# HGRN2 score levels: the two finest ones written after the value projection, apart from the others, with the transposes between them and one shared buffer

## The chip, the cores and the metric

The kernel runs on one core of a Trainium2 chip. A core has a matrix engine (TensorE; PE for its matmuls, PEld for the loads of the stationary operand), a vector engine (VectorE; DVE), a scalar engine (ScalarE; ACT), GpSimd (POOL) and SyncE (SP), which only starts transfers. The metric is the device time of one execution in microseconds (us), lower is better; the kernel before is given by the median of three runs.

## What is computed

One layer of a decoder trunk for 1024 prompt tokens and 64 sample tokens (8 sequences of 8), so 1088 columns in all. Four token mixers share one input projection, and an MLP follows. The change touches one of the four, HGRN2, a gated linear recurrence with four heads of 128 x 128 state. From the reference, cut:

```python
def step(s, inp):
    qi, ki, fi, vi = inp
    b = jnp.cumsum(fi, axis=2)
    o_inter = jnp.einsum("bhtd,bhdv->bhtv", qi * jnp.exp(b), s)
    diff = b[:, :, :, None, :] - b[:, :, None, :, :]
    decay = jnp.exp(jnp.where(causal, diff, -jnp.inf))
    scores = jnp.sum(qi[:, :, :, None, :] * ki[:, :, None, :, :] * decay, axis=-1)
    o = o_inter + jnp.einsum("bhts,bhsv->bhtv", scores, vi)
    b_last = b[:, :, -1:, :]
    s_new = jnp.exp(b_last[:, :, 0, :])[..., None] * s + \
        jnp.einsum("bhsd,bhsv->bhdv", ki * jnp.exp(b_last - b), vi)
    return s_new, o
```

The decay depends on the channel, so the scores of a chunk are not one product of two matrices.

## The kernel before

**Stages.** Tokens lie along the free axis, channels on the 128 partitions. A first stage norms and modulates the input into `Hh` and `Hl`, the high and low parts of a two-part split. The mixer stage follows, up to about 1475 us of the trace, then the branch products, the output product and the MLP. Each projection (`gemm`, L174) is 8 k-blocks x 3 column chunks x 3 products (high-high, low-high, high-low), 72 matmuls of some 363 columns, all recorded on the helper line L107 with the tiles `pg<-Hh,whi` and so on. Its weights come in two halves, each loaded by SP into `wst`, copied by ACT into `whi` and subtracted by DVE into `wlo`.

**Order.** The mixer stage has four rounds, `ROUNDS` (L1087): a string of letters, each of which runs one step of a generator. `r` is a step of RWKV-7, `h` of HGRN2, `c` and `l` of the two convolution branches, `g` a gate projection as filling work, `a` a piece of the conditioning. A round ends in `...h...g h h` (in the last one with the letters a little moved), so each head of HGRN2 has four steps: the q projection; the f projection and all levels of scores; the V projection; the output-gate projection and the rest. What is written is not the final order: at compile time a scheduler puts the instructions of each engine in order, by the place in the program as priority (weights and evacuations of projections have a higher one), whatever is ready by its own model of times first. On the chip each engine then takes its list strictly in that order.

**`hg_block` (L755), one call for each head.** After the projections, `b` (tile `hlf`) is the running sum of the log decay by chunks of 128 tokens (scan, L774). The 128 x 128 scores of a chunk are built by levels. For the level `hs` the chunk falls into groups of `2*hs` tokens, and a tile `X` holds, in the lower half of each group, `exp(b_ref - b) * k`, in the upper half `exp(b - b_ref) * q`, with `b_ref` the value at the group's middle: two DVE subtracts (L809, L810), one ACT exp (L811), two DVE products (L812, L813). A product of the two halves then gives the scores across the middle. Levels 64 and 32 go to the PSUM tiles `l64` and `l32` and by ACT into `P` (tile `hP`). Levels 16, 8, 4, 2 and the two base cases (tokens with themselves and with their neighbour) go through `small_level` (L784): 64 or 68 matmuls of 32 columns each into a PSUM tile `lv`, and one or two predicated copies of DVE (L791, L794) into `acc` (tile `hacc`). When all levels are in, POOL copies the diagonal blocks of `acc` into `P` and `Ps` (L834, L836).

After the next two projections the rest follows: `eb = exp(b)`, `q *= eb` (L847), the decayed keys `kd` (L848 to L854), then a loop over `c0` = 0, 4, 8 (L859) that transposes `V` and `kd` by TensorE into the PSUM tile `htr` (L867, L868), copies them by ACT to `VT`, multiplies `VT` with `P` into `po` and with itself into the state sums `hs`, and carries the state `hS` through four chunks by DVE.

**Buffers.** `flat(name, slot)` (L117) gives one of 13 buffers of 128 x 1120 floats; two tiles with one slot share it, and the later waits until all readers of the earlier are done. The slots of `X` are 3, 12, 7, 3, 12, 7 for the levels 64 to 2. `VT` has 7, 3, 7 for `c0` = 0, 4, 8; the output `hy` has 12. PSUM tiles of `pmt` (`lv`, `l64`, `l32`, `htr`, `hs`) share three banks.

Of the kernel before, what the change touches and what calls it, by code (L numbers as in the profile page):

```python
# [14 lines left out]
OP = mybir.AluOpType  # L15
# [6 lines left out]
NT = T + NS * TS  # L22
# [68 lines left out]
class Net:  # L91
# [70 lines left out]

    def products(self, ps, n0, n, W, X, k0, kt, nk=4):

        hi, lo = W
        xh, xl = X
        for k in range(k0, k0 + nk):
# [5 lines left out]

    def gemm(self, ap, kt, X, evac, chunks=CHUNKS):  # L174
        pss = [None] * len(chunks)
        for k0 in range(0, kt, 4):
            W = self.weights(ap[:, k0:k0 + 4, :])
            for i, (n0, n) in enumerate(chunks):
                if k0 == 0:
                    pss[i] = self.pgt("pg")  # L180
                self.products(pss[i], n0, n, W, X, k0, kt)
                if k0 + 4 == kt:
                    with self.tc.high_priority(offset=PRIO):
                        evac(pss[i], n0, n)

    def gemm_quarters(self, parts, X, evac, groups):


        pss = [None] * len(groups)
        xh, xl = X  # L190
        for j, (ap, ks) in enumerate(parts):
# [563 lines left out]
    def hg_block(self, h):  # L755
        nc = self.nc
        lb, om = self.hlb[:, 8 + h:9 + h], self.hlb[:, 12 + h:13 + h]
        q, f, k = (self.flat(n, i) for n, i in (("hq", 4), ("hf", 1), ("hk", 2)))
# [18 lines left out]
        acc = self.hp.tile([128, 9, 32], F32, name="hacc")  # L777
        P_t = self.flat("hP", 10)
        P = P_t[:, 0:T].rearrange("p (c t) -> p c t", t=128)
        Ps = P_t[0:64, T:NT]  # L780
# [18 lines left out]
        nc.gpsimd.tensor_copy(x1[:, ev], k[:, ev])  # L799
        self.tt(x1[:, od], q[:, od], f[:, od], OP.mult)  # L800
        small_level(4, x1, x1, True)
        for hs in (64, 32, 16, 8, 4, 2):
            N = NT if hs <= 4 else T
            v = lambda a: a[:, :N].rearrange("p (g t) -> p g t", t=2 * hs)
            ng = N // (2 * hs)
            X = self.flat("X", {64: 3, 32: 12, 16: 7, 8: 3, 4: 12, 2: 7}[hs])
            lo, hi = slice(0, hs), slice(hs, 2 * hs)
            ref = v(b)[:, :, hs - 1:hs].to_broadcast([128, ng, hs])
            self.tt(v(X)[:, :, lo], ref, v(b)[:, :, lo], OP.subtract)  # L809
            self.tt(v(X)[:, :, hi], v(b)[:, :, hi], ref, OP.subtract)  # L810
            self.act(X[:, :N], X[:, :N], AF.Exp)  # L811
            self.tt(v(X)[:, :, lo], v(X)[:, :, lo], v(k)[:, :, lo], OP.mult)  # L812
            self.tt(v(X)[:, :, hi], v(X)[:, :, hi], v(q)[:, :, hi], OP.mult)  # L813
            if hs == 64:
                ps = self.pmt("l64")
                for c in range(8):
                    o = c * 128
                    self.mm(ps[0:64, c * 64:c * 64 + 64], X[:, o:o + 64], X[:, o + 64:o + 128])
                self.act(P[0:64, :, 64:128], c3(ps[0:64, :]))
            elif hs == 32:  # L820
                ps = self.pmt("l32")
                for c in range(8):
                    for g in range(2):
                        o = c * 128 + 64 * g
                        self.mm(ps[64 * g:64 * g + 64, c * 32:c * 32 + 32], X[:, o:o + 64], X[:, o + 32:o + 64])
                for g in range(2):
                    R = slice(64 * g, 64 * g + 32)
                    self.act(P[R, :, 64 * g + 32:64 * g + 64], ps[R, :256].rearrange("p (c t) -> p c t", t=32))
            else:
                small_level(HLV.index(hs), X, X, hs <= 4)  # L830

        for g in range(4):
            R = slice(32 * g, 32 * g + 32)
            nc.gpsimd.tensor_copy(P[R, :, R], acc[R, 0:8, :])  # L834
            if g < 2:
                nc.gpsimd.tensor_copy(Ps[R, R], acc[R, 8, :])  # L836

        yield
        V = self.flat("hV", 6)
        self.proj(8 + h, lambda ps, n0, n: self.act(V[:, n0:n0 + n], ps[:, :n]))  # L840
# [3 lines left out]

        eb = self.flat("eb", 1)
        self.act(eb[:, :NT], b[:, :NT], AF.Exp)
        self.tt(q[:, :NT], q[:, :NT], eb[:, :NT], OP.mult)  # L847
        kd = self.flat("kd", 9)  # L848
        for sl, L in ((slice(0, 1024), 128), (slice(1024, NT), 8)):
            v = lambda a: a[:, sl].rearrange("p (c t) -> p c t", t=L)  # L850
# [3 lines left out]
        self.tt(kd[:, :NT], kd[:, :NT], k[:, :NT], OP.mult)  # L854

        ident = self.c("ident")
        y = self.flat("hy", 12)
        S = None
        for c0 in (0, 4, 8):  # L859
            w = 4 if c0 < 8 else 1  # L860
            VT = self.flat("VT", (7, 3, 7)[c0 // 4])[:, :1024].rearrange("p (c a t) -> p c a t", a=2, t=128)
            for c in range(c0, c0 + w, 2):
                ps = self.pmt("htr")
                if c < 8:
                    for cc in range(2):
                        o = (c + cc) * 128
                        nc.tensor.transpose(ps[:, cc * 256:cc * 256 + 128], V[:, o:o + 128], ident)  # L867
                        nc.tensor.transpose(ps[:, cc * 256 + 128:cc * 256 + 256], kd[:, o:o + 128], ident)  # L868
                    self.act(VT[:, c - c0:c - c0 + 2].rearrange("p c a t -> p (c a t)"), ps)
                else:  # L870
                    nc.tensor.transpose(ps[0:64, 0:128], V[:, 1024:NT], ident)
                    nc.tensor.transpose(ps[0:64, 128:256], kd[:, 1024:NT], ident)
                    self.act(VT[0:64, 0].rearrange("p a t -> p (a t)"), ps[0:64, :256])
            po = self.py.tile([128, 512], F32, name="po", tag="py")
            if c0 < 8:
                for c in range(c0, c0 + 4):
# [4 lines left out]
            if c0 < 8:  # L881
# [3 lines left out]
                for c in range(c0, c0 + 4):  # L885
# [8 lines left out]
                    S = Sn  # L894
# [657 lines left out]
```

## Time and profile before

| what | us |
| --- | --- |
| median of 3 runs | 2525.07 |
| the three runs | 2525.07, 2526.18, 2517.87 |
| the profiled execution | 2528.64 |
| its span, first to last instruction | 2526.9 |

The page of the profile gives the busy time of each engine over the span, the span in 40 slices, the transfers by queue, the chain of work that ended last, and the costliest groups of instructions. Other views answer questions on the same trace: waits of an engine by what ended them, instructions in order of time (neighbours of one kind merged into one row, with the idle time before it in brackets and what ended that), and the busy time of the engines in chosen stretches with the TensorE clock that was granted there (1.00 is full speed). "issue" as the end of a wait means that the engine waited for nothing that the profile shows. A matmul's end is modelled and matmuls overlap, so the pace of TensorE is read from the distance of their starts.

The four calls of `hg_block` have their levels at about 383 to 410, 719 to 750, 1060 to 1090 and 1406 to 1438 us of the span. They are called rounds 0 to 3 below.

### The profile page before, as it was taken

Reading aid. Unit: us, or ns where it says so; the run is one execution under the profiler, and the core shown is the slowest. Engines: PE = TensorE matmul, PEld = TensorE weight load, DVE = VectorE, ACT = ScalarE, POOL = GpSimd, SP = SyncE. Lnnn points to the kernel's source line nnn. Section 1 sums busy time; section 2 is a strip of 40 time slices with the busy share of each in tenths; the row PEclk is TensorE's granted clock in tenths of the full one; section 3 lists DMA queues with packets and bytes.
Section 4 is the critical chain, followed back from the end, with each engine's and each line's share of the span. In section 5 each row is a group of like instructions: output and inputs, shape, how many; then the busy total and the mean of one; then the engine's idle time right before and its main releaser. Section 6 shows DMA issues by size and latency. Waiting matters only on the chain.

```text
span 2526.9 us, 46611 instructions
## 1 busy us (share of the span) xinstructions
PE 2430.2 (96%) x19086; PEld 2255.0 (89%) x19086; DVE 1381.1 (55%) x2536; ACT 1037.1 (41%) x1855; POOL 330.2 (13%) x503
## 2 busy tenths in 40 slices
PE   6999999999999999999999999998899999999996
PEld 2897899898888988989888899998899999999996
DVE  6664626637365555457553667668755552422247
ACT  4512434323454235442244653346666665111115
POOL 3101210103100021101012000000222221000003
PEclk9999999999999999999999999999999999999998
DMA  6323132223221232112313455533565557434144
GB/s 242 120 85 91 56 104 68 70 74 98 92 68 63 81 97 97 68 62 80 98 60 105 163 186 169 194 114 104 157 157 157 157 153 257 137 139 184 61 158 132
DMA packets 185111, 300.46 MB, mean 119 GB/s; under 512 B 57385, under 2 KB 97273, under 8 KB 184897
## 3 DMA queue, kind: packets, MB, share of 16 engines
q1 hardware_dynamic: 134480, 217.79, 27.1%
q0 software_dynamic: 47104, 74.44, 9.7%
q10 hardware_dynamic: 3312, 5.25, 0.6%
q8 instruction: 150, 2.46, 0.4%
q14 instruction: 65, 0.52, 0.1%
HBM read 211.29 MB, written 81.66 MB: 116 GB/s over the span
## 4 chain that ended last, share of the span: by engine, by line
PE 79%; DVE 9%; DMA 6%; issue 3%; ACT 3%; SPq 0%; DVEq 0%; ACTq 0%; POOL 0%; POOLq 0%
PE pg L107 52%; PE pa L107 6%; PE pe L107 4%; PE sm L107 2%; PE pc L107 2%; PE pb L107 2%; PE ada L107 2%; PE pu L107 2%; DMA zx<-At 1%; DVE X L101 1%; DVE wlo L101 1%; PE G L107 1%; DMA adaw<-ada 1%; PE pyr L107 1%; PE po L107 1%
## 5 line engine op out<-in xcount | busy, mean ns | idle before, releaser
L107 PE MATMUL pg<-Hh,whi 128*128 128x362 f32 (+1 forms) x1872 | 631.5, 338 | 3.4 <-ACT Hh L98 3.1
L107 PE MATMUL pg<-Hh,wlo 128*128 128x362 f32 (+1 forms) x1872 | 632.6, 338 | 0.0
L107 PE MATMUL pg<-Hl,whi 128*128 128x362 f32 (+1 forms) x1872 | 625.2, 336 | 0.7 <-DVE Hl L104 0.6
L98 ACT ACTIVATE whi<-wst 128x512 fp32r<-128x512 f32 (+1 forms) x404 | 249.9, 620 | 617.0 <-PE pg L107 542.1
L101 DVE TENSOR_TENSOR wlo<-wst,whi 128x512 fp32r<-128x512 f32 (+1 forms) x404 | 280.3, 695 | 379.6 <-ACT whi L98 378.8
L107 PEld LDWEIGHTS pg<-Hh,whi 128*128 128x128 f32 x1872 | 357.4, 191 | 18.9 <-ACT Hh L98 5.9
L107 PEld LDWEIGHTS pg<-Hh,wlo 128*128 128x128 f32 x1872 | 357.8, 191 | 11.9 <-issue 4.2
L107 PEld LDWEIGHTS pg<-Hl,whi 128*128 128x128 f32 x1872 | 356.8, 191 | 10.1 <-issue 2.5
L107 PE MATMUL pg<-ah,whi 128*128 128x272 f32 x960 | 275.3, 289 | 4.3 <-ACT whi L98 4.3
L107 PE MATMUL pg<-ah,wlo 128*128 128x272 f32 x960 | 276.4, 290 | 0.6 <-DVE wlo L101 0.6
L107 PE MATMUL pg<-al,whi 128*128 128x272 f32 x960 | 273.0, 289 | 0.0
L107 PEld LDWEIGHTS pg<-ah,whi 128*128 128x128 f32 x960 | 180.9, 189 | 5.1 <-ACT whi L98 4.9
L107 PEld LDWEIGHTS pg<-ah,wlo 128*128 128x128 f32 x960 | 181.1, 189 | 1.6 <-DVE wlo L101 1.4
L107 PEld LDWEIGHTS pg<-al,whi 128*128 128x128 f32 x960 | 179.4, 189 | 0.0
L104 DVE SCALAR_TENSOR_TENSOR cacc<-u,pv,cacc 128x1024 f32<-128x1024 f32 x120 | 153.7, 1280 | 2.0
L104 DVE SCALAR_TENSOR_TENSOR R<-pg,mod,R 128x544 f32<-128x544 f32 (+2 forms) x120 | 65.7, 569 | 133.8 <-PE pg L107 133.8
L107 PE MATMUL pg<-yh,whi 128*128 128x362 f32 (+1 forms) x384 | 128.7, 335 | 0.9 <-DVE gt L101 0.9
L107 PE MATMUL pg<-yh,wlo 128*128 128x362 f32 (+1 forms) x384 | 127.5, 332 | 0.0
L107 PE MATMUL pg<-yl,whi 128*128 128x362 f32 (+1 forms) x384 | 127.1, 331 | 0.0
L1177 POOL DMA_DIRECT2D g<-gst x96 | 53.3, 555 | 399.0 <-ACT gst L98 383.5
L98 ACT ACTIVATE gst<-pg 128x362 f32<-128x362 f32 (+1 forms) x96 | 45.3, 472 | 134.8 <-PE pg L107 122.5
L689 POOL TENSOR_SCALAR sp<-St,dec 128x64 f32<-128x64 f32 x60 | 56.1, 935 | 231.0 <-DVE St L104 209.1
(446 smaller groups left out, 4819.3 us busy)
## 6 DMA issues: line engine op xcount, KB each, us to landing
wst<-w SPq DMA_DIRECT2D x136, 256.0 KB, 3.2
wst<-w_in SPq DMA_DIRECT2D x92, 256.0 KB, 2.8
gt<-g SPq DMA_DIRECT2D x32, 544.0 KB, 3.7
wst<-w_gate SPq DMA_DIRECT2D x64, 256.0 KB, 2.9
adaw<-ada SPq DMA_DIRECT2D x32, 512.0 KB, 5.3
ah<-ah POOLq DMA_DIRECT2D x60, 272.0 KB, 2.7
al<-al POOLq DMA_DIRECT2D x60, 272.0 KB, 4.3
ah<-ah SPq DMA_DIRECT2D x30, 544.0 KB, 10.0
```

The costliest lines, as they stand in the source:

```text
L98: return self.nc.scalar.activation(out, in_, func, bias=bias, scale=scale)
L101: return self.nc.vector.tensor_tensor(out, a, b, op=op)
L104: return self.nc.vector.scalar_tensor_tensor(out, a, s, b, op0=op0, op1=op1)
L107: return self.nc.tensor.matmul(out, lhsT, rhs, start=start, stop=stop, skip_group_check=True)
L689: nc.gpsimd.tensor_scalar(sp, St, dec[:, c:c + 1], None, op0=OP.mult)
L1177: nc.gpsimd.dma_start(d[:, n0:n0 + n], t[:, :n])
```

## The change

The body of the loop over levels becomes a function `level(hs)`, and the transposes a function `transposes(c0)`. Levels 64, 32, 16 and 8 stay where they were. Levels 4 and 2 are written after the output-gate projection and the decayed keys: transposes of chunks 0 to 3, level 4, transposes of chunks 4 to 7, level 2, and only then POOL's copies into `P` and `Ps` and the product `q *= eb`. The `X` of level 2 has slot 12 now, that of level 4, and no longer slot 7. The loop over `c0` takes the two `VT` that are already there and transposes only the sample tokens itself. The instructions are the same in kind and number, and so are all sizes.

```diff
-        for hs in (64, 32, 16, 8, 4, 2):
+        def level(hs):
             N = NT if hs <= 4 else T
...
-            X = self.flat("X", {64: 3, 32: 12, 16: 7, 8: 3, 4: 12, 2: 7}[hs])
+            X = self.flat("X", {64: 3, 32: 12, 16: 7, 8: 3, 4: 12, 2: 12}[hs])
...
-        for g in range(4):
-            R = slice(32 * g, 32 * g + 32)
-            nc.gpsimd.tensor_copy(P[R, :, R], acc[R, 0:8, :])
-            if g < 2:
-                nc.gpsimd.tensor_copy(Ps[R, R], acc[R, 8, :])
-
+        for hs in (64, 32, 16, 8):
+            level(hs)
         yield
...
         self.act(eb[:, :NT], b[:, :NT], AF.Exp)
-        self.tt(q[:, :NT], q[:, :NT], eb[:, :NT], OP.mult)
         kd = self.flat("kd", 9)
...
-        y = self.flat("hy", 12)
-        S = None
-        for c0 in (0, 4, 8):
+        def transposes(c0):
             w = 4 if c0 < 8 else 1
             VT = self.flat("VT", (7, 3, 7)[c0 // 4])[:, :1024].rearrange("p (c a t) -> p c a t", a=2, t=128)
             for c in range(c0, c0 + w, 2):
...
+            return VT
+
+        VTs = []
+        for c0, hs in ((0, 4), (4, 2)):
+            VTs.append(transposes(c0))
+            level(hs)
+        for g in range(4):
+            R = slice(32 * g, 32 * g + 32)
+            nc.gpsimd.tensor_copy(P[R, :, R], acc[R, 0:8, :])
+            if g < 2:
+                nc.gpsimd.tensor_copy(Ps[R, R], acc[R, 8, :])
+
+        self.tt(q[:, :NT], q[:, :NT], eb[:, :NT], OP.mult)
+        y = self.flat("hy", 12)
+        S = None
+        for c0 in (0, 4, 8):
+            VT = VTs[c0 // 4] if c0 < 8 else transposes(c0)
```

## The prediction

> **What bounds the kernel now.** I read the page first, then what TensorE waits for, then its instructions in time around the levels, and last the granted clock there.
>
> ```profile
> span 2526.9 us, 46611 instructions
> PE 2430.2 (96%) x19086; PEld 2255.0 (89%) x19086; DVE 1381.1 (55%) x2536; ACT 1037.1 (41%) x1855; POOL 330.2 (13%) x503
> q8 instruction: 150, 2.46, 0.4%
> ```
>
> TensorE is busy for 96% of the span, so the change can only pay by idle or slow time of TensorE; work of DVE, ACT and POOL counts where TensorE waits for it. The third row is wanted below: 150 transfers of instructions, 2.46 MB, so 16.4 KB each. TensorE has 2 x 19086 instructions, and 38172 / 150 = 254: this queue brings TensorE's code in blocks of about 256 instructions.
>
> The waits of TensorE, by line and by what ended them:
>
> ```profile
> PE lv L107 <- issue: 9.2, 5, 3.0
> ...
> PE lv L107 <- DVE X L101: 1.9, 3, 0.8
> ```
>
> So the small-level matmuls `lv` stand idle 9.2 us in five pieces without waiting for any engine, and only 1.9 us for DVE. In order of time the five are these (start, duration, count, and in brackets the idle time before):
>
> ```profile
> 405.52 1.64 PE L107 MATMUL lv<-X 128*32 128x32 f32 x140
> 407.68 0.73 PE L107 MATMUL lv<-X 128*32 128x32 f32 x60 [0.53 <-issue]
> ...
> 720.70 0.77 PE L107 MATMUL lv<-x 128*32 128x32 f32 x67 [0.21 <-DVE x L101]
> 722.45 0.19 PE L107 MATMUL lv<-x 128*32 128x32 f32 x1 [0.98 <-issue]
> ...
> 742.28 1.73 PE L107 MATMUL lv<-X 128*32 128x32 f32 x167
> 747.02 0.66 PE L107 MATMUL lv<-X 128*32 128x32 f32 x33 [3.02 <-issue]
> ...
> 1082.82 2.10 PE L107 MATMUL lv<-X 128*32 128x32 f32 x194
> 1087.33 0.33 PE L107 MATMUL lv<-X 128*32 128x32 f32 x6 [2.41 <-issue]
> ...
> 1430.06 1.40 PE L107 MATMUL lv<-X 128*32 128x32 f32 x132
> 1433.08 0.75 PE L107 MATMUL lv<-X 128*32 128x32 f32 x64 [0.43 <-DVE X L101]
> 1436.15 0.32 PE L107 MATMUL lv<-X 128*32 128x32 f32 x4 [2.32 <-issue]
> ```
>
> Four of the five lie in the run of levels 8, 4 and 2: 64 + 68 + 68 = 200 matmuls, 400 instructions with their loads, at about 12 ns a matmul (167 in 1.73 us is 10). Each time the stall comes at another place of the run, after 140, 167, 194 and 196 matmuls, so it is no operand that is missing. What the places share is their distance (busy time and count of matmuls, between the four stalls):
>
> ```profile
> 407.50:746.00 338.50, 330.76 (x2801) 296.96 (x2802) 183.15 (x324) 133.29 (x245) 45.64 (x72) 0.98 0.26 80
> 746.00:1086.00 340.00, 332.90 (x2801) 299.76 (x2801) 181.28 (x320) 133.19 (x245) 43.86 (x72) 0.97 0.25 79
> 1086.00:1435.00 349.00, 341.37 (x2801) 301.63 (x2800) 194.41 (x340) 153.56 (x272) 44.35 (x78) 0.99 0.28 91
> ```
>
> 2801 matmuls each time, with their loads 5602 instructions, and 22 blocks of 256 are 5632, which leaves 30 for semaphore instructions. I read it so: TensorE eats 400 instructions in about 2.3 us and runs dry at the end of a block, because the next is not there yet. The Trainium skill, "Runtime: NRT & Kernel Launch", section Instruction fetch mechanics, also has blocks of 256 instructions, the next fetched while one executes, but calls the cost of the boundary mostly hidden; by that the stalls would have another cause, which is rival C below. Here the trace differs, with up to 3.02 us at a boundary.
>
> The stall has a second price, the granted clock, the third figure from the end of each row:
>
> ```profile
> 746.00:753.00 7.00, 5.97 (x54) 5.91 (x54) 1.12 (x3) 1.82 (x3) 2.31 (x7) 0.51 0.02 4
> 1087.00:1091.00 4.00, 3.67 (x20) 3.60 (x20) 0.52 (x2) 1.19 (x2) 2.31 (x7) 0.57 0.03 6
> 1435.50:1442.50 7.00, 6.35 (x26) 6.20 (x27) 2.26 (x6) 3.98 (x4) 1.96 (x6) 0.51 0.82 310
> ...
> 405.00:409.00 4.00, 3.41 (x208) 2.80 (x206) 3.86 (x7) 0.00 (x0) 0.00 (x0) 1.00 0.27 87
> ```
>
> After the three long stalls TensorE runs at half clock; after the 0.53 us of round 0 it doesn't. The lost time: (1 - 0.51) x 7 less the 1.02 us in which it stood anyway, x 0.49, is 2.9 us; (1 - 0.57) x 4 = 1.7; 0.49 x 7 less 0.65 x 0.49 is 3.1. Together **7.7 us**. The stalls of the four runs themselves are 0.53 + 3.02 + 2.41 + 2.32 = **8.3 us**.
>
> **The change part by part.** No instruction is added or removed; what changes is order and one buffer.
>
> *The shared buffer.* Level 2 may write slot 12 only when the matmuls of level 4 have read it. So the run of 200 falls apart by a dependency that no order can close: after level 4's matmuls come two subtracts, an exp, two products, and then level 2's. From round 0:
>
> ```profile
> 401.04 1.34 DVE L101 TENSOR_TENSOR X<-hlf 128x544 f32<-128x544 f32 x2
> ...
> 404.15 0.71 DVE L101 TENSOR_TENSOR X<-X,hq 128x544 f32<-128x544 f32 x1
> ...
> 405.39 0.71 DVE L101 TENSOR_TENSOR X<-X,hk 128x544 f32<-128x544 f32 x1
> 406.02 0.72 DVE L101 TENSOR_TENSOR X<-X,hq 128x544 f32<-128x544 f32 x1
> ...
> 400.88 1.12 ACT L98 ACTIVATE X<-X 128x1088 f32<-128x1088 f32 x1 [0.21 <-DVE X L101]
> 402.91 1.10 ACT L98 ACTIVATE X<-X 128x1088 f32<-128x1088 f32 x1
> ```
>
> 1.34 + 1.10 + 0.71 + 0.72 = 3.87 us, and about 0.2 for each of three hand-overs (the 0.21 above): 4.5 us between level 4 and level 2. The most instructions that now stand close are level 8's 128 and level 4's 136, 264 against 400. The nearest row for that is the pair of base cases, 2 x 68 matmuls = 272 instructions, which stalled once in four rounds, 0.98 us. So I keep 0.25 us a round for code: **1.0 us** in all, bounds 0 and 4 x 0.98 = 3.9. With such short bursts I expect no half clock behind them, as after the 0.53 us of round 0.
>
> *What TensorE does in the 4.5 us.* The second set of transposes (eight, 0.11 us apart), state sums, and projection matmuls of the next RWKV step. These are there (busy time and count of the tile `pg` alone, and the pace):
>
> ```profile
> 398.40:405.50 7.10, 6.96 (x41) 6.75 (x41) 0.00 (x0) 0.48 (x1) 1.00 0.36 113
> 408.30:416.70 8.40, 5.61 (x32) 5.24 (x32) 0.60 (x1) 0.62 (x2) 1.00 0.11 35
> 416.70:424.00 7.30, 3.46 (x19) 2.79 (x17) 1.38 (x3) 1.42 (x5) 1.00 0.23 77
> ...
> 414.02 0.27 PE L867 MATMUL htr<-cv,hV 128*128 128x128 f32 x1
> 414.13 0.27 PE L868 MATMUL htr<-cv,kd 128*128 128x128 f32 x1
> ...
> 753.12 0.33 PE L107 MATMUL pg<-Hh,whi 128*128 128x364 f32 x1
> 753.28 0.33 PE L107 MATMUL pg<-Hh,wlo 128*128 128x364 f32 x1
> ```
>
> Of the 4.5 us, 0.9 go to transposes; the other 3.6 us at 0.165 us want 22 matmuls, and 51 run after the levels before. So the gap is covered, but on an in-order list the scheduler chooses beforehand how many matmuls it puts in; where the chain on the chip is longer, TensorE waits at level 2. Before, such waits for `X` were 1.9 us in three of four rounds, up to 0.8. Now three places depend on a fresh chain: level 4, level 2 and `po`. I take 0.35, 0.65 and 0.3 us, **5.2 us** over four rounds; bounds: 0, and 0.8 at each of twelve places, 9.6.
>
> *Behind the waiting instructions.* On DVE the subtracts of level 2 now wait for TensorE, and behind them stand level 2's products, weight halves `wlo` and `hS`. The `wlo` are placed by priority and fit into the 1.1 us of the exp. `q *= eb` leaves its place ahead of the last predicated copies. ACT's copies of `htr` to `VT` move ahead, and `level` has to share three PSUM banks with `htr`; both copies are in the way of nothing but exps, and what that costs is in the new waits above. SP and POOL's transfers keep their order; POOL's copies start after level 2 as before:
>
> ```profile
> 409.58 0.82 POOL L834 COPY hP<-hacc 32x256 f32<-32x256 f32 x2 [25.29 <-DVE hacc L794]
> 410.44 0.44 POOL L836 COPY hP<-hacc 32x32 f32<-32x32 f32 x2
> 410.92 0.83 POOL L834 COPY hP<-hacc 32x256 f32<-32x256 f32 x2
> ...
> 416.71 1.05 PE L107 MATMUL po<-hP,VT 128*128 128x128 f32 x8
> ```
>
> They end at 411.8, and `po` came 5 us later, because transposes, `VT` and `hs` had to come first. My chain for the changed round 0: level 4's products ended at 404.9 (404.15 + 0.71) and move up by the 1.3 us of level 2's subtracts, to 403.6; 0.8 us of matmuls, 4.5 us of chain and 0.8 us again give 409.7 for level 2, against 408.4 before; POOL then ends near 413.1. Since `VT` and `hs` are then ready, `po` can be no later than now. Moving the transposes is thus worth nothing by itself: TensorE had projection work in that time. If that cover were gone, POOL's 2.2 us would stand in TensorE's way, 8.8 us over four rounds.
>
> **The sum.** -8.3 - 7.7 + 1.0 + 5.2 = **-9.8 us**. The profiled execution took 2528.64 (1.7 around its span), 3.6 above the median of the runs; the saving is a difference, so I take it from the median: 2525.07 - 9.8 = **2515.3**.
>
> **The rivals.**
>
> *A: the half clock stays.* The Trainium skill, "TensorE: Matmul & The Clock Gate", section Part 1, lets the clock fall to half after an idle window of about 3.4 us; by that rule stalls of 2.3 to 3.0 us would not cause it. As a mechanism of this kernel: the 32-column matmuls themselves count as idleness, and their number doesn't change. Then the 7.7 us stay: -2.1, **2523**. Against it: round 0 has the same 200 matmuls and 1.00.
>
> *B: the starvation moves.* Levels 8 and 4 land together with the transposes (16 instructions), and the block boundary falls badly: one stall of 2.3 us is left in the four rounds, and the new waits are at their upper bound: -16.0 + 2.3 + 9.6 = -4.1, **2521**.
>
> *C: the stall isn't code*, but belongs to the last matmuls of the finest level. Then it stays with its clock, and the new waits come on top: +5.2, **2530**. The equal 2801 speak against it.
>
> *D: slower.* TensorE has nothing to put between level 4 and level 2: 3.6 us idle in each round, and half clock behind it (7.7 / 3 = 2.6): 4 x 6.2 = 24.8 against 16.0, +8.8, **2534**. It decides where fewer than 22 projection matmuls have their weights at that moment. For it: the serial chain is new. Against it: the 51 matmuls above.
>
> **How the numbers follow.** Forecast 0.64, A 0.08, B 0.12, C 0.08, D 0.08. About 0.3% (7.6 us) is what a measurement of this kernel can tell from no change. Faster: the forecast without the 0.06 in which the new waits take more than I gave them, 0.58. Same: that 0.06 with A, B and C, 0.34. Slower: D, 0.08. The forecast's own range is 2509 (new costs nil) to 2523 (both at their bounds, 13.5 us). With the scatter of the three runs, 8 us from 2517.87 to 2526.18, and A and B the range is 2505 to 2527; C and D, 0.16, are left out.
>
> **What would show it.** Right: `lv` waiting on "issue" falls from 9.2 to 2 us or less; no stretch of half clock right behind the levels; level 4 and level 2 stand as runs of 68 with `htr` and `pg` between them, 4 to 5 us apart; `lv` waiting for DVE grows to 3 to 6 us. Wrong: runs of 130 or more still stalling over 2 us; `pg` missing between the two levels; idle time ahead of `po`.

## The result and the profile after

The changed kernel takes 2555.73 us (median of 4 runs, 2552.71 to 2558.05), beside it the kernel before 2525.62. The ratio is 1.0124, with a 95% interval of 1.0108 to 1.0140: **slower by about 30 us**, where 10 us less were forecast, and outside the range of 2505 to 2527. The profiled execution has a span of 2556.2 us.

The part that was aimed at happened. These are TensorE's waits of the changed kernel (total, times, longest):

```profile
PE zq L107 <- DMA X<-zx: 14.4, 4, 3.8
PE p L107 <- ACT vk L98: 2.2, 3, 1.2
PE lv L107 <- ACT whi L98: 1.9, 1, 1.9
...
PE lv L107 <- DVE X L101: 0.7, 1, 0.7
```

The row "lv <- issue", 9.2 us before, is gone. Behind the levels of rounds 1 and 2 TensorE keeps its full clock, which the third figure from the end of each row of the stretches shows (0.51 and 0.57 before; in round 3 the clock still falls, which the last section shows):

```profile
750.00:770.00 20.00, 20.00 (x318) 19.14 (x317) 14.00 (x32) 9.33 (x21) 2.33 (x7) 1.00 0.22 68
1096.00:1116.00 20.00, 20.00 (x319) 19.14 (x317) 13.96 (x31) 9.07 (x21) 2.33 (x7) 1.00 0.22 68
```

And yet each round ends later. Round 0 of the changed kernel in order of time:

```profile
402.81 0.71 DVE L101 TENSOR_TENSOR X<-X,hq 128x544 f32<-128x544 f32 x1
...
403.95 0.76 PE L107 MATMUL lv<-X 128*32 128x32 f32 x64
...
408.33 0.80 PE L107 MATMUL lv<-X 128*32 128x32 f32 x68
...
410.14 1.35 DVE L101 TENSOR_TENSOR X<-hlf 128x544 f32<-128x544 f32 x2
...
413.37 0.72 DVE L101 TENSOR_TENSOR X<-X,hq 128x544 f32<-128x544 f32 x1
...
416.06 0.80 PE L107 MATMUL lv<-X 128*32 128x32 f32 x68
...
420.12 0.45 POOL L877 COPY hP<-hacc 32x32 f32<-32x32 f32 x2
...
424.88 1.05 PE L107 MATMUL po<-hP,VT 128*128 128x128 f32 x8
```

Level 4's products are done at 403.5, but its matmuls run at 408.33: in TensorE's list eight transposes and 16 projection matmuls stand ahead of them. Level 2's products are done at 414.1, its matmuls run at 416.06, behind 36 projection matmuls. In this stretch TensorE has no recorded wait; it works. `po` itself, whose scores POOL has copied by 420.6, stands behind further projections and comes at 424.88, 8.2 us later than before (416.71).

How that goes on is seen in the square of the output, `hsq`, at the end of each head. The kernel before:

```profile
432.14 1.11 ACT L98 ACTIVATE hsq<-hy 128x1088 f32<-128x1088 f32 x1
...
773.47 1.11 ACT L98 ACTIVATE hsq<-hy 128x1088 f32<-128x1088 f32 x1
...
1112.54 1.11 ACT L98 ACTIVATE hsq<-hy 128x1088 f32<-128x1088 f32 x1
...
1467.79 1.11 ACT L98 ACTIVATE hsq<-hy 128x1088 f32<-128x1088 f32 x1
```

The changed kernel:

```profile
440.02 1.11 ACT L98 ACTIVATE hsq<-hy 128x1088 f32<-128x1088 f32 x1
...
788.18 1.11 ACT L98 ACTIVATE hsq<-hy 128x1088 f32<-128x1088 f32 x1
...
1133.98 1.11 ACT L98 ACTIVATE hsq<-hy 128x1088 f32<-128x1088 f32 x1
...
1498.42 1.11 ACT L98 ACTIVATE hsq<-hy 128x1088 f32<-128x1088 f32 x1
```

Later by 7.9, 14.7, 21.4 and 30.6 us. The way from the scan of `hlf` to `hsq`, the **tail** below, sums to 231.0 us over the four rounds against 213.5: 17.5 of the 30.6. The other 13.1 arise between the tails. What follows the last `po` shows how little is paid back. Each kernel cut there, `pg` matmuls alone (first figures: length, busy time and count); before:

```profile
0.00:1467.20 1467.20, 1043.31 (x5720) 960.80 (x5720) 38.38 (x80) 112.96 (x282) 0.98 0.29 93
1467.20:2526.90 1059.70, 664.89 (x4888) 658.44 (x4888) 135.74 (x296) 11.87 (x24) 0.98 0.50 155
```

After:

```profile
0.00:1497.90 1497.90, 1061.48 (x5826) 975.14 (x5826) 42.87 (x89) 112.56 (x282) 0.97 0.29 93
1497.90:2556.20 1058.30, 654.82 (x4782) 647.94 (x4782) 131.12 (x287) 11.89 (x24) 0.98 0.50 153
```

By the last `po` the changed kernel has done 106 projection matmuls more, 17.5 us of work at 0.1655. The rest should be that much shorter and is shorter by 1.4 us. One execution can't carry this figure to the microsecond: e3 below, whose TensorE list is that of the kernel before, needed 1067.8 us for the rest where the kernel before needed 1059.7. In its first 60 us (all engines) the kernel before has TensorE busy for 59.10 us at a clock of 1.00:

```profile
1467.20:1527.20 60.00, 59.10 (x348) 57.16 (x348) 40.53 (x62) 33.73 (x37) 1.08 (x2) 1.00 0.66 216
```

The changed kernel has 52.29 us at 0.91:

```profile
1497.90:1557.90 60.00, 52.29 (x281) 49.81 (x281) 38.18 (x58) 29.78 (x33) 1.08 (x2) 0.91 0.59 189
```

and of TensorE's waits in these 60 us one row says for what (total, times, longest):

```profile
PE pg L107 <- ACT yh L98: 7.2, 3, 6.2
```

The counts say which work had been drawn forward. By the last `po` every `pg` matmul that reads the input, `Hh` or `Hl`, gates included, is done in both kernels: 5616. The rest are branch products, 104 of them before and 210 in the changed kernel. They are what could have covered the end, and so TensorE stands there for the inputs `yh` of those that are left. The kernel before has no such wait in its 60 us. **The longer rounds were filled with work from a store that was missing later.**

On TensorE the whole loss can be added up. Both kernels run the same 19086 matmuls, and the page of the kernel before has it busy for 2430.2 us of 2526.9; that of the changed kernel has

```profile
PE 2453.1 (96%) x19086; PEld 2264.6 (89%) x19086; DVE 1373.4 (54%) x2536; ACT 1040.9 (41%) x1859; POOL 322.2 (13%) x503
```

of 2556.2. Of the 29.3 us more, 22.9 are busy time for the same matmuls and 6.4 are idle. The mean granted clock of the two executions is 0.981 and 0.974. 0.026 x 2556.2 less 0.019 x 2526.9 gives, as an estimate, 18 us more of withheld clock, so most of the longer busy time is half clock, part of it in the 60 us above (0.91) and in two stretches of 0.89 and 0.71 that are shown below. This says where the time lies, not what put it there.

### The profile page after: what moved, and what is told of

It is laid out like the page before. It is cut to its first block, busy times and chain, and to the rows that moved or that the text cites. A ratio compares the mean times of both kernels' runs of the same rounds, so it can differ in the third digit from the quotient of the medians.

```text
span 2556.2 us, 46614 instructions
## 1 busy us (share of the span) xinstructions
PE 2453.1 (96%) x19086; PEld 2264.6 (89%) x19086; DVE 1373.4 (54%) x2536; ACT 1040.9 (41%) x1859; POOL 322.2 (13%) x503
## 4 chain that ended last, share of the span: by engine, by line
PE 84%; DVE 7%; DMA 5%; ACT 2%; issue 1%; SPq 0%; ACTq 0%; DVEq 0%
PE pg L107 57%; PE pa L107 5%; PE pe L107 3%; PE sm L107 3%; PE pc L107 2%; PE ada L107 2%; PE pb L107 2%; PE pu L107 2%; DMA zx<-At 1%; PE pyr L107 1%; PE G L107 1%; PE po L107 1%; DVE wlo L101 1%; DMA wst<-w 1%; PE pst L107 1%
## 5 line engine op out<-in xcount | busy, mean ns | idle before, releaser
L107 PEld LDWEIGHTS pg<-yh,whi 128*128 128x128 f32 x384 | 74.2, 193 | 12.9 <-ACT yh L98 8.1
```

Of the source, the lines that this page charges most:

```text
L107: return self.nc.tensor.matmul(out, lhsT, rhs, start=start, stop=stop, skip_group_check=True)
```

## The experiments

Four parts of the change can be told apart: the shared buffer, the late writing, the transposes between the levels, and where the tail ends. All kernels compute everything. The planned order of TensorE, known from the compiled program, is counted in the expectations.

**First: one part at a time.** e1 is the changed kernel with a buffer of its own for level 2, e2 the kernel before with the shared buffer:

```diff
# e1, against the changed kernel; e2 has the 7 of before as 12, nothing else
-            X = self.flat("X", {64: 3, 32: 12, 16: 7, 8: 3, 4: 12, 2: 12}[hs])
+            X = self.flat("X", {64: 3, 32: 12, 16: 7, 8: 3, 4: 12, 2: 5}[hs])
# e3, against the changed kernel, with slot 7 for level 2
-        VTs = []
-        for c0, hs in ((0, 4), (4, 2)):
-            VTs.append(transposes(c0))
+        for hs in (4, 2):
             level(hs)
...
-            VT = VTs[c0 // 4] if c0 < 8 else transposes(c0)
+            VT = transposes(c0)
# e4, against the kernel before: POOL's copies twice
+            for _ in range(2):
                 nc.gpsimd.tensor_copy(P[R, :, R], acc[R, 0:8, :])
...
```

> The changed kernel with one number different: level 2 writes slot 5, which is free there, and no longer shares slot 12 with level 4. The transposes stay between the levels. Theory 1 (the tail of the round is late): the serial chain level 4 - level 2 holds back the score copies, `po` and the h tail; each us by which the tail is late, the next RWKV block's vector chain is late too, while projection matmuls were used up earlier. The scheduler's list then tells the price: projection matmuls between level 8 and the last `po`, over those of before, at 0.1655 us. The changed kernel has 57, 48, 48 and 33 more in the four rounds, 186 x 0.1655 = 30.8 us (measured +30). This one has 40, 24, 24 and 6, 94 x 0.1655 = 15.6: about 2541, faster than the changed kernel by 10 to 18 us, slower than before. Rival 2 (the place of the transposes does it: their copies on ACT stand ahead of the exps): no better than the changed kernel, 2550 to 2558. Rival 3 (only the shared buffer does it): back at 2525 or, with the code stalls gone, at 2510.

> The kernel before with one number different: level 2 writes slot 12, shared with level 4. Nothing is moved. Theory 1: 48, 33, 26 and 13 more projection matmuls between level 8 and the last `po`, 120 x 0.1655 = 19.9 us: about 2545 (2537 to 2552). Rival 2 (the transposes' place): no slower than before, 2510 to 2525, since the runs of 200 are broken up and the code stalls go. Rival 3 (only the shared buffer): as the changed kernel, 2550 to 2558.

> Levels 4 and 2, the score copies and `q *= eb` are written where the change has them, but with the buffers of before and with the transposes behind the levels as before. The planned order of TensorE comes out the same as before, instruction for instruction. Theory 1, rival 2 and rival 3: as before, 2525 +- 5. Rival 4 (the late writing itself costs, through the order on DVE, ACT and POOL): slower by 10 us or more.

> The kernel before, with POOL's copies of the scores from `hacc` to `hP` and `Ps` done twice (the second time the same values): 2.2 us more on the way from level 2 to `po` in each round, no work for TensorE, nothing of the change. Theory 1: the tail is late without the change: about 70 more projection matmuls ahead of the last `po` over the four rounds, x 0.1655 = 11.6 us, about 2537 (2531 to 2542). Rival 5 (TensorE alone is the bound, and where the h tail ends costs nothing as long as projections fill): 2525, and where the longer lists break up the runs of small matmuls, up to 10 us less.

| kernel | us (before beside it) | ratio, 95% interval |
| --- | --- | --- |
| e1 own buffer | 2560.41 (2529.40) | 1.0129, 1.0114 to 1.0144 |
| e2 shared only | 2545.19 (2529.40) | 1.0071, 1.0045 to 1.0098 |
| e3 late only | 2529.01 (2529.40) | 1.0001, 0.9988 to 1.0015 |
| e4 copies twice | 2561.06 (2529.40) | 1.0131, 1.0114 to 1.0147 |

Late writing costs nothing (e3, where TensorE's planned order is that of before). The shared buffer alone costs 16 us (e2, as the first theory had it), but beside the transposes it adds nothing: e1 without it is as slow as the changed kernel, so the first theory's 15.6 us for e1 was a miss and rival 2 held. e4 changes nothing of the levels and loses as much: 2.2 us more on POOL in each round cost 32. That a late tail is expensive was right, the size (11.6 us expected) was not.

In e1 both buffers are free, and still the levels wait their turn:

```profile
406.58 0.71 DVE L101 TENSOR_TENSOR X<-X,hq 128x544 f32<-128x544 f32 x1
...
407.20 0.76 PE L107 MATMUL lv<-X 128*32 128x32 f32 x64
...
411.57 0.80 PE L107 MATMUL lv<-X 128*32 128x32 f32 x68
...
416.08 0.80 PE L107 MATMUL lv<-X 128*32 128x32 f32 x68
```

All products are done by 407.3, and level 2's matmuls run at 416.08. What they share with the transposes is the ring of three PSUM banks: level 8, four `htr`, and the two levels between them take turns, each after the copy of the tile three places back.

**Second: banks apart, and POOL's copies on DVE.**

```diff
# f4, against e1 (n = 2 is level 4, n = 3 is level 2)
-            ps = self.pmt("lv")
+            ps = self.pc.tile([128, 512], F32, name="lv", tag="pc") if n == 2 else self.py.tile([128, 512], F32, name="lv", tag="py") if n == 3 else self.pmt("lv")
# g1, against f4; c6, against the changed kernel; part of c4
-            nc.gpsimd.tensor_copy(P[R, :, R], acc[R, 0:8, :])
+            nc.vector.tensor_copy(P[R, :, R], acc[R, 0:8, :])
...
# c4, against the kernel before, with the copies on DVE
-        for hs in (64, 32, 16, 8, 4, 2):
+        for hs in (4, 64, 2, 32, 8, 16):
...
-            X = self.flat("X", {64: 3, 32: 12, 16: 7, 8: 3, 4: 12, 2: 7}[hs])
+            X = self.flat("X", {4: 3, 64: 12, 2: 7, 32: 3, 8: 12, 16: 7}[hs])
```

> The order of the change (level 4 and level 2 late, transposes between them), level 2 in slot 5 as in e1, and in addition the two levels' scores in PSUM banks outside the ring of three: level 4 in the bank of `pu` and `pst`, level 2 in that of `po`. Theory 2 (after e1: the transposes between the levels take the ring's banks, so each level waits for a copy of the tile three places back, and in TensorE's list both stand behind transposes and projection matmuls): with banks of their own the planned list is again 108 projection matmuls from the level-16 scores to the last `po`, as before (changed kernel: 156, 135, 135, 174; e1: 147, 114, 114, 143), and no run of more than 68 small matmuls is left. About 2510 to 2520 against 2529 on that chip: the code stalls and their half clock go, the tail ends as before. Rival 2 as first put (the copies of the transposes on ACT are in the way, not the banks): as e1, 2555 to 2565, since they stand where they stood. Rival 6 (TensorE's order between the levels is not what costs): 2545 or more.

> As f4, and the score copies from `hacc` to `hP` and `Ps` on DVE in place of POOL (POOL takes 0.41 to 0.44 us for each of six). The planned list falls to 84 projection matmuls in rounds 0 to 2 (108 in f4 and before). Theory 1: an earlier tail is worth at least what the list says, 24 x 0.1655 = 4.0 us a round over three rounds, 12 us below f4: about 2500 (2490 to 2510). Rival 7 (a late tail costs, but an early one brings nothing, since then the RWKV block waits for its own projections): as f4 within 4 us.

> The changed kernel with the score copies on DVE in place of POOL, nothing else. List from the level-16 scores to the last `po`: 145, 117, 117, 150 (changed kernel 156, 135, 135, 174; before 108, 108, 108, 153). Theory 1: 11, 18, 18 and 24 matmuls fewer, 71 x 0.1655 = 11.8 us, and, as e4 showed a late tail to cost more than its own length, up to 25: 2533 to 2548 against 2559 for the changed kernel on that chip. Rival 8 (the place of the transposes is what costs, wherever the tail ends): 2553 to 2562.

> The kernel before with the order of the levels 4, 64, 2, 32, 8, 16 (slots 3, 12, 7, 3, 12, 7) and the score copies on DVE; transposes stay behind all levels. No run of more than 64 + 16 small matmuls is left in rounds 0 to 2, and the list has 117 projection matmuls with the window beginning one level earlier. Theory 1 with the code stalls: the stalls and their half clock go (16 us), the tail ends no later: 2505 to 2518. Rival: mixed levels bring new waits on DVE, 2525 to 2535.

| kernel | us (before 2528.33) | ratio, 95% interval | last `po` | from there to the end |
| --- | --- | --- | --- | --- |
| f4 banks apart | 2523.69 | 0.9985, 0.9972 to 0.9997 | 1457.6 | 1062.5 |
| g1 f4, copies on DVE | 2524.66 | 0.9984, 0.9972 to 0.9997 | 1452.9 | 1076.6 |
| c6 change, copies on DVE | 2558.57 | 1.0112, 1.0093 to 1.0131 | 1498.1 | 1056.1 |
| c4 mixed levels | 2517.79 | 0.9951, 0.9936 to 0.9966 | 1457.0 | 1059.0 |

f4 differs from e1 only in two PSUM banks, and 36 us are gone. In its order of time level 4 runs ahead of level 8, as soon as its products are there, and level 2 right behind the first transposes:

```profile
400.61 0.71 DVE L101 TENSOR_TENSOR X<-X,hq 128x544 f32<-128x544 f32 x1
...
401.46 0.79 PE L107 MATMUL lv<-X 128*32 128x32 f32 x68 [0.42 <-DVE X L101]
...
407.19 0.76 PE L107 MATMUL lv<-X 128*32 128x32 f32 x64
...
408.90 0.80 PE L107 MATMUL lv<-X 128*32 128x32 f32 x68
```

So the ring, not the copies on ACT, is what the transposes did to the levels. The gain that f4 was to bring, 9 us or more, did not come (4 us). c4 is the fastest kernel of this study and came in its range.

The first theory fell with g1 and c6: both missed its ranges, and rivals 7 and 8 held. g1's tails are 18.8 us shorter than f4's in sum (187.3 against 206.1), and it is no faster. Cut at the last `po`, `pg` matmuls alone:

```profile
0.00:1452.90 1452.90, 1030.87 (x5672) 951.51 (x5672) 36.20 (x76) 112.62 (x282) 0.98 0.29 93
1452.90:2529.50 1076.60, 677.17 (x4936) 671.44 (x4936) 138.06 (x300) 11.87 (x24) 0.98 0.49 153
```

Its last `po` is 4.7 us earlier than f4's, the rest 14.1 longer, of which 24 matmuls not yet done are 4.0. Part of the 14.1 belongs to this execution, which took 2531.29 us against g1's median of 2524.66. And c6 has tails of 52.3 us in rounds 1 and 2, as short as before (53.0 and 51.2), and stays slow. Its four tails are 5.8 us longer in sum, and its last `po` is 30.9 us later: most of its loss arises between the tails. There the slow kernels have a hole. The tile `zq` belongs to RWKV-7 and is made ahead of its recurrence. From the last `zq` to the first state of the recurrence, rounds 1 and 2, `pg` alone; before:

```profile
550.00:578.90 28.90, 18.66 (x105) 17.21 (x105) 1.66 (x4) 1.42 (x3) 1.00 0.47 129
891.30:920.10 28.80, 18.67 (x105) 17.22 (x105) 1.66 (x4) 1.42 (x3) 1.00 0.49 129
```

The changed kernel, with 76 and 32 matmuls in place of 105, and a clock of 0.89 and 0.71:

```profile
558.60:590.20 31.60, 14.09 (x76) 12.43 (x76) 1.67 (x4) 0.00 (x0) 0.89 0.43 128
909.30:938.40 29.10, 6.14 (x32) 5.20 (x32) 0.00 (x0) 0.00 (x0) 0.71 0.34 87
```

**Third: a step or a slope.** In f4's plan the hole opens between two and three repeated copies.

```diff
# x1: n = 2, x2: n = 3, against f4; x3: n = 2, z2: n = 4, against the kernel before
+            if g < n:
+                nc.gpsimd.tensor_copy(P[R, :, R], acc[R, 0:8, :])
             nc.gpsimd.tensor_copy(P[R, :, R], acc[R, 0:8, :])
```

c2 is c4 with its copies on POOL.

> f4 (banks apart) with two of the four score copies on POOL done twice: 0.8 us more ahead of `po` in each round, the same values. Theory 3 (after c6 and g1): what counts is where the list puts the projection matmuls. From the end of the h tail's list to the start of the next recurrence they are filler; in the kernels that are not slower the stretch from `zq` to the first state of the recurrence has 98 to 105 of them, in the slower ones 13 to 81. This list has 190 in the tail, 504 up to `zq`, 98 behind it, in all rounds: as f4 within 4 us, about 2527. Theory 1 (each us of a later tail costs 3 to 4, as e4 had it): 4 x 0.8 x 3.6 = 11 us over f4, 2535.

> As x1 with one copy more, three of the four done twice: 0.41 us more ahead of `po` in each round than x1. The list, though, falls over: 196, 522, 74 in the first round, then 177, 545, 31, and 177, 545, 98. Theory 3: a step, not a slope: slower than x1 by 15 to 30 us, 2543 to 2558. Theory 1: 4 x 0.41 x 3.6 = 6 us over x1 at most, 2541 or less, and by the copy's own length only 1.6 us.

> The kernel before with two of the four score copies on POOL done twice, as x1 on its base. List: 180, 508, 104 in the first three rounds (before: 168, 519, 105): no hole behind `zq`. The run of 200 small matmuls stays whole in rounds 0 to 2. Theory 3: as before within 5 us, 2523 to 2534, where e4 with all copies twice (list with 85, 31, 88 behind `zq`) was at +32. Theory 1: a quarter to a half of e4, +8 to +16 us.

> The kernel before with the order of the levels 4, 64, 2, 32, 8, 16 (slots 3, 12, 7, 3, 12, 7), nothing else: c4 without its copies on DVE. List 171, 516, 105: full behind `zq`. No run of more than 64 + 16 small matmuls in rounds 0 to 2. Theory 3 with the code stalls: the stalls and their half clock go and nothing is given back: 2512 to 2520, as c4. If the gain of c4 came from the copies on DVE: 2525 to 2532.

| kernel | us (before 2527.35) | ratio, 95% interval | last `po` | from there to the end |
| --- | --- | --- | --- | --- |
| x1 f4, two copies more | 2523.52 | 0.9981, 0.9967 to 0.9994 | 1451.8 | 1071.5 |
| x2 f4, three copies more | 2556.96 | 1.0111, 1.0087 to 1.0135 | 1498.9 | 1055.2 |
| x3 before, two copies more | 2520.74 | 0.9969, 0.9956 to 0.9982 | 1454.9 | 1062.2 |
| c2 mixed levels | 2523.72 | 0.9981, 0.9970 to 0.9992 | 1456.3 | 1062.6 |

One copy more in each round, 0.41 us off TensorE, costs **33 us**. It is a step. Two copies more cost nothing, on either base; x3, with more work than before, is even 0.31% faster, below its range. x1 and x2 came in the third theory's ranges; c2 came between its two (2512 to 2520, 2525 to 2532), so a good half of c4's gain hangs on its copies on DVE. Cut at the last `po`, `pg` alone, x1 and then x2:

```profile
0.00:1451.80 1451.80, 1031.18 (x5712) 952.72 (x5712) 38.37 (x80) 112.68 (x282) 0.99 0.29 94
1451.80:2523.40 1071.60, 674.24 (x4896) 668.72 (x4896) 136.00 (x296) 11.88 (x24) 0.98 0.49 153
```

```profile
0.00:1498.90 1498.90, 1052.96 (x5773) 968.30 (x5773) 40.76 (x85) 112.32 (x282) 0.97 0.29 92
1498.90:2554.20 1055.30, 658.10 (x4835) 653.17 (x4835) 133.41 (x291) 11.87 (x24) 0.98 0.50 154
```

x2's tails are only 4.2 us longer than x1's in sum, and its last `po` is 47 us later: nearly all of it arises between the tails, where TensorE has the same matmuls in another planned order.

**Fourth: is the hole the cause?** With the same h block, another place of one step among the gates fills it in the plan.

```diff
# y1, against the changed kernel, rounds 1 and 2
-'rragrggchgcagllgghghh'
+'rragrggchgcgallgghghh'
# y2, against the changed kernel; y3, against the kernel before; y4, against c4
-'rragrggchgcagllgghghh'
+'rragrggcahgcgllgghghh'
```

> The changed kernel; only the order of the steps of rounds 1 and 2 differs, in two letters: the gate comes ahead of the second ada step ('...hgcga...' for '...hgcag...'). The h block is untouched. Planned projection matmuls: tail 216, 203, 194 (changed kernel 216, 195, 195), from there to `zq` 518, 469, 462 (518, 540, 540), behind `zq` 130, 103, 101 (76, 13, 90). Theory 3 (the hole is the cause: projections that it can't take must run where TensorE is the bound): 0 + 71 + 78 = 149 matmuls fewer ahead of `zq` x 0.1655 = 24.7 us, about 2532 (2525 to 2542). Theory 2 alone (the longer tail behind the PSUM ring is what costs): the tails are as long as in the changed kernel, 2548 to 2560.

> The changed kernel; in rounds 1 and 2 the second ada step stands ahead of the h projection, and a gate stands in its old place ('...ggcahgcg...' for '...ggchgcag...'). Planned: tail 216, 195, 194; ahead of `zq` 453, 477, 462; behind it 161, 159, 103. Theory 3: 65 + 63 + 78 = 206 matmuls fewer ahead of `zq` x 0.1655 = 34 us at most, 2522 to 2535. Theory 2 alone: 2548 to 2560.

> The kernel before with the order of y2, as its control. Planned ahead of `zq` 479, 474, 536 (before 519 in each), behind it 168, 159, 105 (105, 105, 123), recurrences 610, 626, 520 (576, 576, 521). Theory 3: 68 fewer ahead of `zq`, -11 us, and 84 more in the recurrences, +14 us if TensorE is their bound and 0 if it is the chain: 2516 to 2531, so y2's gain over the changed kernel is not simply that of a better order. If the order of the steps alone is worth 25 us or more whatever the tail: 2500 or less.

> c4 (mixed levels, score copies on DVE) with the order of y2. Planned ahead of `zq` 471, 483, 508 (c4 509 in each), behind it 161, 175, 105, recurrences 614, 605, 520 (576, 576, 521). Theory 3: -65 x 0.1655 = -11 us, and up to +11 in the recurrences: 2505 to 2518, c4 or a little below.

| kernel | us (before 2527.93) | ratio, 95% interval |
| --- | --- | --- |
| y1 change, gate first | 2583.87 | 1.0222, 1.0199 to 1.0246 |
| y2 change, gate earlier | 2584.35 | 1.0233, 1.0213 to 1.0253 |
| y3 before, gate earlier | 2553.45 | 1.0108, 1.0087 to 1.0130 |
| y4 mixed, gate earlier | 2575.88 | 1.0194, 1.0176 to 1.0212 |

All four missed. In y2 the hole is full and the clock there 1.00 (the same two stretches, `pg` alone):

```profile
562.70:599.10 36.40, 28.92 (x161) 26.32 (x161) 1.67 (x4) 1.42 (x3) 1.00 0.26 75
921.40:957.60 36.20, 28.68 (x160) 26.08 (x160) 1.67 (x4) 1.41 (x3) 1.00 0.28 82
```

and it is slower than the changed kernel by 28 us. Against its control y3 it loses 31 us, as the changed kernel does against the kernel before. The cut is not a clean one: the moved step brings a wait of its own, for the transfers of the conditioning. The changed kernel, then y2:

```profile
PE ada L107 <- DMA adaw<-ada: 16.6, 3, 15.3
```

```profile
PE ada L107 <- DMA adaw<-ada: 27.5, 8, 15.4
```

This is 11 of the 25 us by which y2's TensorE is longer idle. Its busy time, though, is that of the changed kernel (2453.6 us against 2453.1), so the full hole has won nothing. The third theory falls as the account of the loss: filling the hole does not bring the time back. Why the order of the steps alone costs the kernel before 25 us (y3) was not followed further.

**Fifth: the fourth corner, and the step on the kernel before.** z1 has f4's line of banks in the changed kernel.

> The changed kernel with the scores of level 4 and level 2 in PSUM banks of their own, as f4; the buffer of the two levels stays shared. With the changed kernel (shared, ring), e1 (own, ring) and f4 (own, banks apart) this is the fourth corner. Planned projection matmuls up to the last `po` of the last round: 4364 (before 4280, f4 4256, e1 4355, changed kernel 4386); the kernels as fast as before have 4232 to 4284, the slow ones 4320 to 4386. Theory 4 (what is lost is told by how much filler the planned list uses up in the four rounds, wherever it stands): slow, 2545 to 2560. Rival (only the ring costs, the shared buffer is free once the ring is gone): as f4, 2520 to 2530.

> The kernel before with all four of POOL's large score copies done twice, 1.6 us more ahead of `po` in each round; x3 had two of them, 0.8 us more. Planned projection matmuls up to the last `po`: 4346 (x3 4278, before 4280). Theory 4: a step again, 2545 to 2560, 25 us or more above x3. A slope by the copies' own length: 4 x 0.8 = 3 us above x3, 2524 or so.

| kernel | us (before 2525.53) | ratio, 95% interval | last `po` | from there to the end |
| --- | --- | --- | --- | --- |
| z1 change, banks apart | 2549.71 | 1.0098, 1.0073 to 1.0123 | 1489.2 | 1053.2 |
| z2 before, four copies more | 2563.75 | 1.0146, 1.0121 to 1.0170 | 1498.4 | 1057.0 |

z1 came in the range of theory 4; z2 was slower, as theory 4 had it, but 4 us above its range. Each of the two parts suffices: with the ring out of the way the shared buffer still costs, and of the four corners only f4, with buffer and banks both apart, is not slow. And the step is there on the kernel before too, between x3 and z2. The count of the fourth theory, projection matmuls planned up to the last `po`, separates all kernels: 4232 to 4284 in those that are not slower, 4320 to 4386 in the slow ones (executed, from the start of the span: 5672 to 5724 and 5760 to 5826). It doesn't rank them (y1 and y2 have 4386 like the changed kernel and are 28 us slower). Nor is it a measure of filling in all four rounds: every one of the kernels has done the 5616 matmuls on the input by then, and the count differs only by the branch products, 56 to 108 and 144 to 210. It tells how late the last tail ends among them.

What is shown, then: the change makes each tail longer in TensorE's planned order, by the shared buffer and by the PSUM ring, either of which is enough; the whole planned order of the rounds turns to a longer one in a step; and only about half of the work drawn forward is paid back at the end. From the last `po` on the twelve kernels whose interval lies wholly above 1 need 1053 to 1063 us, 1057.8 on average, and the eight others 1059 to 1077, 1065.3 on average. That is 7.5 us less, for 88 matmuls done earlier, which are 14.5 us of work. All twelve wait for `yh` there, 1.4 to 8.8 us, and none of the eight does. **Left open** is which choice of the planner turns first between x1 and x2, and by which waits the time between the tails grows.

One more difference goes with the two groups. ACT loads a table (`ACT_TABLE_LOAD`, 1.28 us each) 50 to 52 times in the eight and 54 to 58 times in the twelve; the changed kernel has 54, the kernel before 50. Four loads are 5.1 us of ACT, so by their own length they can't make the 30 us. Whether they delay the rounds was not tested.

## Why the prediction was wrong, point by point

- **The code stalls, -8.3, and the half clock behind them, -7.7: right in mechanism.** "lv <- issue" fell from 9.2 to 0. Rival C (not code) falls: the last stall of c2, in the last section, comes at the same place of TensorE's list as one of before, ahead of the 8500th matmul, though the levels stand in another order. Rival A (the small matmuls alone bring the half clock) falls with the clock of 1.00 behind the levels of rounds 1 and 2. But what the stalls and the half clock were worth is not shown. f4 has no stall at its levels, waits only 1.8 us for `X`, has no longer plan, and is 0.15% faster, 4 us of the 16 (interval 1 to 7). It pays in other places: a stall of 1.2 us on a projection and a wait of 2.7 us of its transposes for `VT`. x3 keeps 7.4 us of "lv <- issue" and is 0.31% faster than before. And of the 7.7 us, the 3.1 of round 3 did not go: the changed kernel has a clock of 0.66 over 10 us there, by a wait of another kind, about as much again. Of the residual stalls I had kept 1.0 us, none came in the changed kernel.
- **"`po` can be no later than now": the step that failed, and with it the term of the sum that stood at nothing.** It was 8.2 us later in round 0. I followed operands: level 2 at 409.7, POOL done at 413.1. Measured were 416.9 (416.06 and 0.80 for its matmuls) and 420.6. The chain from level 4's matmuls to level 2's was 7.7 us in place of 0.8 + 4.5, and level 4 itself ran at 408.33, not 403.6, for no operand's sake. I had named the three banks, and put their price into the new waits, as though they could only make TensorE stand. The ring gave the levels later places in its list instead (e1 against f4). The 5.2 us of new waits were in truth 2.6 ("lv <- whi" and "lv <- X"), and the lateness, which I priced at nothing, was 17.5 us in the tails and 13.1 between them.
- **"TensorE had projection work in that time": true, and no comfort.** 36 matmuls stood between the two levels, more than the 22 that I asked for, so rival D's mechanism, TensorE idle in the gap, didn't occur, although its sign did. Work that fills a gap is free only if it need not be there later. Here 106 matmuls, 17.5 us of work, were drawn forward and bought 1.4 us at the end in the two executions shown.
- **"The change can only pay by idle or slow time of TensorE"**, from its 96%: this made me cost the end of the h tail at zero. As an account it even holds, since the loss is idle and slow time of TensorE. But I looked for new idle and slow time at the levels only, and it arose elsewhere. The busy share says nothing on which chain sets the rounds' length; e4, and x2 against x1, which add work to POOL alone, show it at 32 and 33 us.
- **Rival B** (stalls return at another boundary) had no part in it: the changed kernel has no wait on "issue" at its levels.
- **"No instruction is added or removed"** holds for the program as written. The page has 1859 instructions on ACT in place of 1855; the four are table loads.
- **What was to show it:** "lv" runs of 68 with `htr` and `pg` between them came, but 7.7 us apart in place of 4 to 5, and the waits of `lv` for DVE did not grow (0.7). These were the signs that the levels were late by order and not by operand. None of the signs of being wrong that I had listed came, so the list could not have warned of it.

## What to carry to other kernels

Where a scheduler writes the order beforehand, a change is first read in its planned lists: count the filling work ahead of the next step of the chain, since one extra dependency or one shared bank in a ring can turn the whole order (here 0.41 us more on POOL in each round cost 33). Filling work is a finite store: before calling a gap covered, look where that work would have stood, and whether the end of the kernel can shrink by it. When a change with several parts loses, try the corners: here the loss went away with two lines that keep buffer and banks apart (f4, 4 us faster than before), and mixing coarse and fine levels gained 5 us, or 12 with the copies on DVE (c2, c4).

## What the runs showed of the hardware that was not expected

The clock of TensorE fell with less idle time than in the long stalls before, which were 2.3 to 3.0 us. In round 3 of the changed kernel there was a wait of 1.88 us between two bursts of small matmuls, and over the 10 us that hold it the clock was 0.66:

```profile
1448.08 1.12 PE L107 MATMUL l<-X 128*64 128x32 f32 x32 [0.39 <-DVE X L101]
...
1451.09 1.08 PE L107 MATMUL lv<-X 128*32 128x32 f32 x64 [1.88 <-ACT whi L98]
```

```profile
1448.00:1458.00 10.00, 7.55 (x116) 7.37 (x117) 10.00 (x18) 8.06 (x10) 0.00 (x0) 0.66 0.46 155
```

The Trainium skill, "TensorE: Matmul & The Clock Gate", section Part 1, has the clock fall after an idle window of about 3.4 us; here the idle pieces are 0.39 and 1.88 us, so either the small matmuls count as idleness in part, or less idleness than a whole window is enough. No run here tells the two apart. What speaks against small matmuls alone is round 0 of the kernel before: 200 of them, 0.53 us of idle time and a clock of 1.00. And the stall at a code boundary needs less than the 400 instructions of the old run. In c2, round 2, 32 matmuls of `l` and 128 of `lv` stand close together, 320 instructions with their loads, and the last ten of them come late:

```profile
1076.03 1.12 PE L107 MATMUL l<-X 128*64 128x32 f32 x32
1077.08 1.28 PE L107 MATMUL lv<-X 128*32 128x32 f32 x118
1080.54 0.28 PE L107 MATMUL lv<-X 128*32 128x32 f32 x10 [2.17 <-issue]
```

The first of the ten is the 8500th matmul of TensorE's list, and in the kernel before the late six of round 2, at 1087.33, begin with the 8500th too. My estimate that 264 instructions are nearly safe has thus a thin margin.
